# adaLN sums: half of the products moved from VectorE to ScalarE, their additions to GpSimd

## The chip, the cores and the metric

One NeuronCore of a Trainium2 chip runs the whole program. The metric is the device time of one execution in microseconds. Three executions of the kernel before took 2615.36, 2617.19 and 2618.43 us. Besides these, one execution was recorded by the hardware profiler.

The engines are named as in the profile: PE is TensorE (PEld its weight loads), DVE is VectorE, ACT is ScalarE, POOL is GpSimd, SP is SyncE, whose queue issues all the DMA transfers spoken of here.

## The reference

Two layers of a diffusion backbone work on 1024 latent tokens and 256 context tokens, 1024 features each. The part that the change touches is the modulation of each layer by a condition:

```
def _adaln(cond, w, b):
    m = jax.nn.silu(cond) @ w + b
    shift, scale, gate = jnp.split(m[:, None, :], 3, axis=-1)
```

There are two conditions: `c` for the latent tokens and `c_ctx` for the context tokens. The matrix `w_mod` of a layer is 1024 x 3072. So each adaLN product is two rows times a large matrix, a sum over 1024 rows of weights for 3072 columns, twice. The first layer then multiplies the normalised tokens by a matrix of 1024 x 7696 (`w_in_ab`), whose columns feed windowed attention and a bidirectional matrix memory (mLSTM) with its gates, and a second layer follows with latent attention.

## The kernel before, in words

The program's first 60 us compute the shift and scale of layer 0 and the modulated tokens, transposed, as a high and a low part (`hTh`, `hTl`), since a product of 32-bit numbers is made of three matmuls of reduced form. Then PE runs the dense projections block by block (`Dense`, `DenseBlock`, `Unit`): a block is 256 columns of `w_in_ab`, and a unit is one output tile of it, 24 matmuls (8 steps over the 1024 features, three matmuls each) into one PSUM bank, tile `S`. The blocks in the stretch of interest are, in order: the values and gate columns (`a_values`, 10 units with 272 columns, up to 90 us), two blocks of the first memory head that are convolved (`qk_block`: units of 512 and 256 tokens, 90 to 161 us), its values (`v_split`, from 161 us) and its output gates (`o_tanh`, from 195 us).

The weights of a block are split before use: `DenseBlock.split` lets ACT cast a weight tile to the high part `wh` (L354), and POOL subtracts to get the low part `wl` (L355). A block has eight `wl`. Twelve buffers exist (`bufs` 6, times two), so the first four `wl` of a block are made while the block before still runs, and the last four wait until it is nearly done with its own. They fall at the transition from block to block.

The rest of adaLN that does not need to be early (layer 0's gate, layer 1's shift and scale) is computed beside these blocks by `mod_steps`, in six column groups of 512. For each group, eight weight tiles of 128 x 512 (`mw`, four buffers, loaded by SP) are multiplied with one condition value per partition and summed into `macc`, which has a half for each condition: `cd` 0 is `c`, `cd` 1 is `c_ctx`. The first tile is a multiplication (L319), each further one a multiply-and-add on DVE (L321), once for each condition. At the end a matmul with two selecting columns adds up the 128 partitions (`total`), and DVE adds the bias (`bmod`, L306). `Dense.stream` advances this one step for every matmul unit or so. Two groups run beside `a_values` and the first convolved block (67 to 100 us), four beside the next three blocks (150 to 220 us). Later in the program four more groups of 256 columns are summed by the same function.

Between the two, `gates` turns the gate columns (`gt`) into the memory's scaling vectors: a logarithm's series on DVE, transposes of `GI` and `GF` on PE, four kinds of scan along the tokens on DVE (L1371 to L1378), the vectors `LF` and `LI` (L1400, L1401), exponentials on ACT (L1406 to L1413), and transposes of `LI`, `rst` and `gM` back on PE (L107).

In this part of the program the order of the instructions on each engine is set by the framework's scheduler, which plans with its own assumed durations; each engine then works its own list strictly in order and waits where an input is not there. From about 235 us on the order is the program's own (`manual_schedule`).

Of the kernel before, what the change touches and what calls it, by code (L numbers as in the profile page):

```python
# [10 lines left out]
F32 = mybir.dt.float32  # L11
# [3 lines left out]
ALU = mybir.AluOpType  # L15
# [128 lines left out]
def body(tc, I, O, dbg=None, stop_at=None):  # L144
    K = Kern(tc, I, O, dbg)
    with ExitStack() as ctx:
        K.const = ctx.enter_context(tc.tile_pool(name="const", bufs=1))
        K.dram = ctx.enter_context(tc.tile_pool(name="dram", bufs=1, space=DRAM))
        K.left = lambda n: tc.alloc_tile_pool(name=n, bufs=1, side="left", reuse_waits="tile")
        K.right = lambda n: tc.alloc_tile_pool(name=n, bufs=1, side="right", reuse_waits="tile")  # L150
        K.set_psum(S=6, T=2)
        setup_consts(K)
        layer_ab(K)
        layer_c(K)
        K.set_psum()
# [130 lines left out]
def mod_steps(K, p, blocks, ahead, width=512):  # L286


    nc = K.nc
    parts = [(l, f, k) for l, f in blocks for k in range(KD)]  # L290
    asked = []

    def ask():
        if parts:
            l, f, k = parts.pop(0)
            w = K.t(p, [128, width], F32, "mw", ahead)
            K.dma(w, K.I["w_mod"][l, k * 128:(k + 1) * 128, f:f + width])
            asked.append(w)

    def total(l, f, acc):  # L300
        ps = K.ps()
        for cd in range(2):
            K.mm(ps[0:2, 0:width], K.sel[cd], acc[:, cd], cd == 0, cd == 1)
        bm = K.t(p, [2, width], F32, "bmod", 1)
        K.dma(bm, K.I["b_mod"][l:l + 1, f:f + width].to_broadcast([2, width]))
        nc.vector.scalar_tensor_tensor(bm, ps[0:2, 0:width], 0.5, bm, ALU.mult, ALU.add)  # L306
        K.dma(K.modd[l][:, f:f + width], bm)

    for _ in range(ahead):
        ask()  # L310
    late = None
    for l, f in blocks:
        acc = K.t(p, [128, 2, width], F32, "macc", 2)
        for k in range(KD):
            w = asked.pop(0)
            for cd in range(2):
                c = K.condT[:, cd * KD + k:cd * KD + k + 1]
                if k == 0:
                    nc.vector.tensor_scalar(acc[:, cd], w, c, None, ALU.mult)  # L319
                else:  # L320
                    nc.vector.scalar_tensor_tensor(acc[:, cd], w, c, acc[:, cd], ALU.mult, ALU.add)  # L321
            ask()
            if late and k == 5:
                late()
                late = None
            yield
        late = partial(total, l, f, acc)
    if late:
        late()
# [320 lines left out]
def layer_ab(K):  # L650
    nc, I = K.nc, K.I
# [36 lines left out]
    dense = Dense(blocks)  # L688
# [47 lines left out]
    zs[3].parts = 4  # L736
    mp = left("mod")
    dense.mods = mod_steps(K, mp, mods[0:2], 4)
    K.tp = gtp = left("gtmp")
    dense.run(1, 1)  # L740
# [4 lines left out]
    mp.release()  # L745
    mp = left("mod1")
    dense.mods = mod_steps(K, mp, mods[2:], 4)
    dense.run(3, 0.9)
    for _ in dense.mods:
        pass  # L750
    mod_cols(K, 1, mp)
# [5 lines left out]
    w = I["w_out_ab"][0]  # L757
# [40 lines left out]
    p = left("wo2")  # L798
# [1114 lines left out]
def layer_c(K):  # L1913
# [23 lines left out]
    nc.vector.tensor_scalar(ncol[:, 0:3], ps[:, 0:3], QSC, None, ALU.mult)  # L1937
    nc.vector.tensor_copy(ncol[:, 3:5], ps[:, 3:5])
    dense.mods = mod_steps(K, cm, [(1, 2 * D + f) for f in range(0, D, 256)], 4, 256)
    dense.run(3, 0.8)  # L1940
    for _ in dense.mods:
# [412 lines left out]
```

## Time and profile before

| | |
|---|---|
| median of three executions | 2617.19 us |
| profiled execution, its time | 2614.64 us |
| its span in the profile | 2612.8 us |
| granted TensorE clock, mean | 0.997 |
| instructions | 48325 |

The span is the time from the first to the last recorded instruction; 1.8 us of the profiled execution's time lie outside it. Times of rows count from the span's start. In a row of the timeline stand the start, the length, the engine, the line, the operation with its output and inputs, and how many instructions it merges; in square brackets how long the engine had been idle before and what ended this. A row of the windows gives for one stretch the busy time of each engine with the number of its instructions, the clock, and the share of the DMA engines. A row of the waits names the waiting engine and line, what it waited for, the total, the number of times and the longest.

### The profile page before, as it was taken

What the parts mean: (1) busy time and instruction counts of PE and PEld (TensorE: products, weight loads), DVE (VectorE), ACT (ScalarE), POOL (GpSimd) and SP (SyncE); (2) the same over time, 40 slices, a digit from 0 to 9 for tenths busy, and PEclk for the clock granted to TensorE, in tenths of its full rate; (3) what the DMA queues carried; (4) which work ended last, traced back from release to release, by engine and by line L of the source; (5) the groups of instructions that cost most, each with busy time, mean ns of one, the idle gap of its engine ahead of it and who ended that gap; (6) DMA issues with size and microseconds to landing.
All of it is one profiled execution on the core that took longest, in us unless ns stands there. A gap on an engine that the chain in (4) does not pass through costs nothing. (4 is left out here: it accounts for less than half of the span.)

```text
span 2612.8 us, 48325 instructions
## 1 busy us (share of the span) xinstructions
PE 2563.6 (98%) x16233; PEld 2259.4 (86%) x16233; DVE 1779.5 (68%) x4045; ACT 1411.7 (54%) x3608; POOL 1161.8 (44%) x1549
## 2 busy tenths in 40 slices
PE   7999999999999999999999999999999999999998
PEld 6888898898898888887888878898899989999887
DVE  6994565656647676477777546526788888888754
ACT  5232444444434433477666433234788888888842
POOL 4342333423324344356445453224455545555832
PEclk9999999999999999999999999999999999999999
DMA  7565576566667664445443453523310101101333
GB/s 249 155 183 174 163 208 189 160 197 188 179 199 212 204 211 153 135 150 161 120 126 106 130 193 133 160 73 101 88 36 27 45 27 38 36 28 29 120 99 131
DMA packets 352970, 347.23 MB, mean 133 GB/s; under 512 B 36073, under 2 KB 297878, under 8 KB 352466
## 3 DMA queue, kind: packets, MB, share of 16 engines
q1 hardware_dynamic: 352722, 344.14, 43.2%
q8 instruction: 129, 2.11, 0.3%
q14 instruction: 119, 0.97, 0.1%
HBM read 233.52 MB, written 110.51 MB: 132 GB/s over the span
## 5 line engine op out<-in xcount | busy, mean ns | idle before, releaser
L355 POOL TENSOR_TENSOR wl<-wf,wh 128x256 fp32r<-128x256 f32 (+3 forms) x288 | 241.7, 864 | 435.8 <-ACT wh L354 381.2
L103 PE MATMUL mm<-hTh,wh 128*128 128x512 f32 (+1 forms) x912 | 329.0, 361 | 0.9 <-DVE scr L621 0.9
L103 PE MATMUL mm<-hTh,wl 128*128 128x512 f32 (+1 forms) x912 | 325.1, 356 | 0.0
L103 PE MATMUL mm<-hTl,wh 128*128 128x512 f32 (+1 forms) x912 | 325.0, 356 | 0.0
L103 PE MATMUL S<-cK,cQ 96*128 96x512 f32 (+3 forms) x1248 | 296.9, 364 | 2.2 <-ACT cPa L2256 1.3
L2304 DVE TENSOR_TENSOR cpl<-T,cph 128x512 fp32r<-128x512 f32 x336 | 228.6, 686 | 45.9 <-ACT cph L2303 42.8
L103 PEld LDWEIGHTS S<-cK,cQ 96*128 96x128 f32 (+1 forms) x1248 | 193.3, 189 | 25.4 <-ACT cPa L2256 3.5
L2303 ACT CAST cph<-T 128x512 fp32r<-128x512 f32 x336 | 192.4, 591 | 29.8 <-PE T L107 18.6
L103 PEld LDWEIGHTS mm<-hTh,wl 128*128 128x128 f32 x912 | 171.7, 188 | 26.6
L103 PEld LDWEIGHTS mm<-hTh,wh 128*128 128x128 f32 x912 | 171.6, 188 | 24.9 <-DVE scr L621 1.1
L103 PEld LDWEIGHTS mm<-hTl,wh 128*128 128x128 f32 x912 | 171.7, 188 | 23.2
L2254 DVE TENSOR_REDUCE cmx<-S 128x1 f32<-128x512 f32 x256 | 173.2, 682 | 16.7 <-PE S L103 15.2
L103 PE MATMUL V<-cph,cV 128*128 128x256 f32 x672 | 177.2, 290 | 1.1 <-DVE co L2319 0.8
L103 PE MATMUL V<-cpl,cV 128*128 128x256 f32 x672 | 172.1, 284 | 0.3 <-DVE cpl L2304 0.3
L1174 ACT CAST att_ph<-mm 128x512 fp32r<-128x512 f32 x168 | 98.6, 587 | 102.0 <-PE mm L107 100.7
L2235 POOL TENSOR_SCALAR cPa<-cPa,cst 128x512 f32<-128x512 f32 x128 | 98.7, 771 | 118.2 <-DVE cst L2232 97.6
L354 ACT CAST wh<-wf 128x256 fp32r<-128x256 f32 (+3 forms) x288 | 101.8, 409 | 74.9 <-DMA wf<-in_w_in_ab 42.8
L103 PE MATMUL mm<-wh,hTh 128*128 128x256 f32 x480 | 136.9, 285 | 4.0 <-DVE scr L1488 4.0
L1175 DVE TENSOR_TENSOR att_pl<-mm,att_ph 128x512 fp32r<-128x512 f32 x168 | 115.8, 689 | 34.8 <-ACT att_ph L1174 29.2
L1163 POOL TENSOR_SCALAR att_p<-att_p,att_den 128x640 f32<-128x640 f32 (+1 forms) x128 | 97.4, 774 | 86.9 <-DVE att_den L1160 39.1
L103 PE MATMUL mm<-wl,hTh 128*128 128x256 f32 x480 | 135.3, 282 | 0.1
L103 PE MATMUL mm<-wh,hTl 128*128 128x256 f32 x480 | 135.3, 282 | 0.0
(456 smaller groups left out, 7887.6 us busy)
## 6 DMA issues: line engine op xcount, KB each, us to landing
wf<-in_w_in_ab SPq DMA_DIRECT2D x120, 256.0 KB
in<-in SPq DMA_DIRECT2D x40, 514.0 KB
in<-in SPq DMA_DIRECT2D x32, 386.0 KB
mw<-in_w_mod SPq DMA_DIRECT2D x48, 256.0 KB
in<-scr SPq DMA_DIRECT2D x40, 258.0 KB
o_x<-y SPq DMA_DIRECT2D x20, 512.0 KB
wm<-in_w_mod SPq DMA_DIRECT2D x16, 512.0 KB
in<-cx SPq DMA_DIRECT2D x32, 256.0 KB
```

The lines of the kernel that those rows point to most:

```text
L103: return self.nc.tensor.matmul(out, lhsT, rhs, start=start, stop=stop)
L354: K.nc.scalar.copy(wh, wf[:, k])
L355: K.nc.gpsimd.tensor_sub(wl, wf[:, k], wh.bitcast(F32))
L1163: nc.gpsimd.tensor_scalar(pv, pv, den[:, i:i + 1], 1.0, ALU.mult, ALU.mult)
L1174: K.nc.scalar.copy(ph, self.T)
L1175: K.nc.vector.tensor_sub(pl, self.T, ph.bitcast(F32))
L2235: nc.gpsimd.tensor_scalar(pv, pv, wt[:, c:c + 1], rd, ALU.mult, ALU.mult)
L2254: nc.vector.tensor_reduce(mx[:, b, c:c + 1], S, AX.X, ALU.max, negate=True)
L2303: nc.scalar.copy(ph, T_)
L2304: nc.vector.tensor_sub(pl, T_, ph.bitcast(F32))
```

## The change

In `mod_steps`, for groups of 512 columns and from the second weight tile on, the second condition's multiply-and-add on DVE becomes two instructions: ACT multiplies the weight tile by the condition's value into a new tile `mq` (two buffers), and POOL adds `mq` to `macc`. The first condition stays on DVE, and so do the first tiles and the groups of 256 columns. The second hunk changes only a blank. All lines behind the change have numbers higher by four.

```diff
                 if k == 0:
                     nc.vector.tensor_scalar(acc[:, cd], w, c, None, ALU.mult)
+                elif cd == 0 or width < 512:
+                    nc.vector.scalar_tensor_tensor(acc[:, cd], w, c, acc[:, cd], ALU.mult, ALU.add)
                 else:
-                    nc.vector.scalar_tensor_tensor(acc[:, cd], w, c, acc[:, cd], ALU.mult, ALU.add)
+                    q = K.t(p, [128, width], F32, "mq", 2)
+                    nc.scalar.mul(q, w, c)
+                    nc.gpsimd.tensor_add(acc[:, cd], acc[:, cd], q)
...
-    dense.run(3, 0.9)
+    dense.run(3,0.9)
```

In the built program 42 multiply-and-adds (six groups, seven tiles) leave DVE's list, and 42 `ACTIVATE` and 42 `TENSOR_TENSOR` enter ACT's and POOL's. The scheduler also moves other instructions. Three places matter. In the rows a number behind a tile's name tells its buffers apart.

The first is POOL's list around the start of the first convolved block, where the last four `wl` of that block are made (`wl_763` to `wl_775`). Before, they follow the clearing of the gate vectors:

```order
L1368 MEMSET gB 36x1280
L1369 MEMSET gM 36x1280
L355 TENSOR_TENSOR wl_763<-wf_750,wh_762 128x256
L355 TENSOR_TENSOR wl_767<-wf_750,wh_766 128x256
L355 TENSOR_TENSOR wl_771<-wf_760,wh_770 128x256
L355 TENSOR_TENSOR wl_775<-wf_760,wh_774 128x256
```

Now:

```order
L325 TENSOR_TENSOR macc_906<-macc_906,mq_1264 128x512
L325 TENSOR_TENSOR macc_1284<-macc_1284,mq_1319 128x512
L325 TENSOR_TENSOR macc_1284<-macc_1284,mq_1358 128x512
L325 TENSOR_TENSOR macc_1284<-macc_1284,mq_1473 128x512
L325 TENSOR_TENSOR macc_1284<-macc_1284,mq_1492 128x512
L325 TENSOR_TENSOR macc_1284<-macc_1284,mq_1550 128x512
L325 TENSOR_TENSOR macc_1284<-macc_1284,mq_1574 128x512
L325 TENSOR_TENSOR macc_1284<-macc_1284,mq_1611 128x512
L359 TENSOR_TENSOR wl_763<-wf_750,wh_762 128x256
L359 TENSOR_TENSOR wl_767<-wf_750,wh_766 128x256
L359 TENSOR_TENSOR wl_771<-wf_760,wh_770 128x256
L359 TENSOR_TENSOR wl_775<-wf_760,wh_774 128x256
```

All fourteen additions of the first two groups (the last eight are shown) stand between the clearing and `wl_763`. On ACT the fourteen products stand ahead of the casts that make `wh_762` to `wh_774`.

The second is PE's list around the first transpose of the gates' result, `LI`, which DVE makes at the end of the scans. Before, it stands in the second convolved block (its weights are `wh_1202` and on):

```order
L103 MATMUL S_1720<-hTh_131,wl_1207 128x512
L103 MATMUL S_1720<-hTh_131,wh_1212 128x512
L103 MATMUL S_1720<-hTl_132,wh_1212 128x512
L107 MATMUL T_1474<-small,LI 128x36 x10
L103 MATMUL S_1720<-hTh_131,wl_1213 128x512
L103 MATMUL S_1720<-hTh_131,wh_1216 128x512
L103 MATMUL S_1720<-hTl_132,wh_1216 128x512
```

Now it stands 40 rows earlier, in the last unit of the first convolved block:

```order
L103 MATMUL S_1614<-hTh_133,wl_763 128x256
L103 MATMUL S_1614<-hTh_133,wh_766 128x256
L103 MATMUL S_1614<-hTl_134,wh_766 128x256
L107 MATMUL T_1496<-small,LI 128x36 x10
L103 MATMUL S_1614<-hTh_133,wl_767 128x256
L103 MATMUL S_1614<-hTh_133,wh_770 128x256
L103 MATMUL S_1614<-hTl_134,wh_770 128x256
```

Every row of PE below it can start only when `LI` is there. The transposes of `rst` and `gM` move up by 43 rows, the first of `GI` by 16 and the first of `GF` by 35.

The third is POOL's list at the transition to the memory's values, where the last four `wl` of that block are made. Before (`cx` is a convolution's middle tap):

```order
L1465 TENSOR_SCALAR cx_1753<-scr_1713,cw 128x512
L1465 TENSOR_SCALAR cx_1762<-scr_1749,cw 128x512
L1465 TENSOR_SCALAR cx_1807<-scr_1803,cw 128x256
L1465 TENSOR_SCALAR cx_1889<-scr_1848,cw 128x512
L1465 TENSOR_SCALAR cx_1898<-scr_1885,cw 128x512
L355 TENSOR_TENSOR wl_1660<-wf_1647,wh_1659 128x256
L355 TENSOR_TENSOR wl_1664<-wf_1647,wh_1663 128x256
L355 TENSOR_TENSOR wl_1668<-wf_1657,wh_1667 128x256
L355 TENSOR_TENSOR wl_1672<-wf_1657,wh_1671 128x256
```

Now the same four are called `wl_1688` to `wl_1700`:

```order
L1469 TENSOR_SCALAR cx_1843<-scr_1839,cw 128x256
L325 TENSOR_TENSOR macc_1916<-macc_1916,mq_1992 128x512
L325 TENSOR_TENSOR macc_1916<-macc_1916,mq_2068 128x512
L325 TENSOR_TENSOR macc_1916<-macc_1916,mq_2104 128x512
L1469 TENSOR_SCALAR cx_1931<-scr_1888,cw 128x512
L325 TENSOR_TENSOR macc_1916<-macc_1916,mq_2140 128x512
L1469 TENSOR_SCALAR cx_1940<-scr_1927,cw 128x512
L359 TENSOR_TENSOR wl_1688<-wf_1675,wh_1687 128x256
L359 TENSOR_TENSOR wl_1692<-wf_1675,wh_1691 128x256
L325 TENSOR_TENSOR macc_1916<-macc_1916,mq_2166 128x512
L359 TENSOR_TENSOR wl_1696<-wf_1685,wh_1695 128x256
L359 TENSOR_TENSOR wl_1700<-wf_1685,wh_1699 128x256
```

Twelve additions of the third and fourth group (four of them shown) now stand between the first convolution `cx` of the second block and `wl_1688`, and a thirteenth between `wl_1692` and `wl_1696`. PE's list first uses these four 11, 10, 22 and 22 rows later than before.

## The prediction

> **What bounds the kernel now.** I read the page's busy times first, then a table of stretches, then PE's waits, then single rows. PE is busy almost throughout, so a change pays only by what it does to PE's waits and clock.
>
> ```profile
> PE 2563.6 (98%) x16233; PEld 2259.4 (86%) x16233; DVE 1779.5 (68%) x4045; ACT 1411.7 (54%) x3608; POOL 1161.8 (44%) x1549
> ```
>
> The products lie between 67 and 220 us. The windows of that stretch (columns: stretch, length, PE, PEld, DVE, ACT, POOL, clock, DMA share, GB/s):
>
> ```profile
> 70.00:94.00 24.00, 24.00 (x177) 23.08 (x176) 22.72 (x49) 4.44 (x13) 4.17 (x4) 1.00 0.86 260
> 124.00:146.00 22.00, 17.96 (x104) 14.45 (x103) 20.65 (x35) 8.24 (x14) 17.99 (x11) 0.97 0.33 83
> 146.00:168.00 22.00, 22.00 (x135) 19.68 (x135) 21.18 (x38) 4.24 (x10) 7.15 (x7) 0.96 0.61 171
> 168.00:194.00 26.00, 24.64 (x189) 21.93 (x188) 22.57 (x46) 7.85 (x22) 8.48 (x8) 1.00 0.78 238
> ```
>
> DVE is nearly full there and ACT and POOL have room. Yet PE waits little: these are all of its waits from 60 to 260 us.
>
> ```profile
> PE T L107 <- ACT rst L1410: 2.2, 1, 2.2
> PE T L107 <- DVE LI L1401: 1.6, 1, 1.6
> PE S L103 <- POOL wl L355: 0.2, 1, 0.2
> PE S L103 <- DVE bmod L306: 1.4, 1, 1.4
> ```
>
> They make 5.4 us, and one has a sequel. The timeline around the two gate transposes:
>
> ```profile
> 132.18 0.40 PE L103 MATMUL S<-hTl,wh 128*128 128x512 f32 x1
> 134.19 0.78 PE L107 MATMUL T<-small,LI 36*128 36x36 f32 x10 [1.61 <-DVE LI L1401]
> 140.12 0.28 PE L103 MATMUL S<-hTh,wh 128*128 128x256 f32 x1
> 140.24 0.28 PE L103 MATMUL S<-hTl,wh 128*128 128x256 f32 x1
> 142.76 0.80 PE L107 MATMUL T<-small,rst 36*128 36x36 f32 x10 [2.23 <-ACT rst L1410]
> 145.07 0.41 PE L103 MATMUL S<-hTl,wh 128*128 128x256 f32 x1
> 145.28 0.41 PE L103 MATMUL S<-hTh,wl 128*128 128x256 f32 x1
> 148.10 0.39 PE L103 MATMUL S<-hTh,wl 128*128 128x512 f32 x1
> ```
>
> Before the wait for `rst` matmuls of 256 start 0.12 us apart, behind it 0.21; from about 144.5 to 147.9 us the array ran at about half rate, which costs half of 3.4 us, 1.7 us. So everything that this stretch can give back is 5.4 + 1.7 = 7.1 us. That is the bound on the good side.
>
> **The change: the durations.** Rows for each kind of work: DVE's multiply-and-adds, a POOL addition of 128x512 and an ACT activation of that shape elsewhere in the program, and four meetings of POOL with DVE.
>
> ```profile
> L321 DVE SCALAR_TENSOR_TENSOR macc<-mw,condT,macc x84: 728/747/1303, 70.2 to 218.9; 128x512 f32<-128x512 f32 x84
> 70.21 3.39 DVE L321 SCALAR_TENSOR_TENSOR macc<-mw,condT,macc 128x512 f32<-128x512 f32 x5
> L909 POOL TENSOR_TENSOR w<-w,o_x x38: 1273/1292/1680, 1525.8 to 2595.5; 128x512 f32<-128x512 f32 x38
> L1471 ACT ACTIVATE scr<-cx x48: 416/632/637, 107.6 to 707.0; 128x512 f32<-128x512 f32 x32, 128x256 f32<-128x256 f32 x16
> 223.75 2.80 POOL L355 TENSOR_TENSOR wl<-wf,wh 128x256 fp32r<-128x256 f32 x4 [12.77 <-ACT wh L354]
> 89.55 4.17 POOL L355 TENSOR_TENSOR wl<-wf,wh 128x256 fp32r<-128x256 f32 x4 [20.76 <-ACT wh L354]
> 89.95 3.17 DVE L321 SCALAR_TENSOR_TENSOR macc<-mw,condT,macc 128x512 f32<-128x512 f32 x3
> ```
>
> Five multiply-and-adds in a row take 3.39 us, 0.67 each from start to start, so the 42 taken from DVE are worth 42 x 0.67 = 28 us of DVE. ACT gets 42 x 0.63 = 26 us, POOL 42 x 1.29 = 54 us, and both have room for it on average. But POOL and DVE hold each other up: four `wl` alone take 0.70 us each (223.75), beside DVE's sums 1.04 (89.55), and DVE's sums there 1.06 instead of 0.67. One of each takes 1.05 us per pair against 0.70 + 0.67 = 1.37 in sequence: 0.32 us overlaps, the rest excludes the other. For an addition of 512 beside a sum I work out a pair of 1.29 + 0.67 - 0.32 = 1.64 us. So an addition lasts between 1.29 us (DVE elsewhere) and about 1.64 us (DVE summing), and DVE is held up by up to 1.64 - 0.67 = 0.97 us for each product that it saved 0.67 on. Where DVE is busy throughout, the move frees nothing of it.
>
> The Trainium skill, "SBUF — State Buffer", section "Who interferes with whom", says that a VectorE instruction with two SBUF inputs and a GpSimd instruction that reads SBUF share a read port, and that the later one is blocked for the whole of the other. The trace agrees that they exclude each other, but 1.05 us per pair is less than the sum of both. By the rule as written a pair here would last 1.96 us; what that gives is the third rival below.
>
> **First transition, 90 us: no wait.** PE's first need of a late `wl` is this one:
>
> ```profile
> 93.46 0.39 PE L103 MATMUL S<-hTh,wl 128*128 128x512 f32 x1
> ```
>
> The fourteen additions can begin when the first products do, at about 70 us. They last 14 x 1.29 = 18 to 14 x 1.64 = 23 us, so POOL is free for `wl_763` between 88 and 93 us, and it is there by 94. The scheduler has moved PE's use of it behind five more matmuls of 0.23 us, to 94.6. I take no wait; up to 1.5 us is possible, since ACT's casts of `wh` stand behind the products, and each product behind the addition two before it.
>
> **The gates: 2.0 us lost.** DVE's chain to `LI` and `rst`:
>
> ```profile
> 95.03 0.17 DVE L921 COPY gt<-S 128x16 f32<-128x16 f32 x1
> 97.51 0.86 DVE L1320 TENSOR_TENSOR gt<-gt,gb 128x160 f32<-128x160 f32 x1
> 98.29 1.22 DVE L321 SCALAR_TENSOR_TENSOR macc<-mw,condT,macc 128x512 f32<-128x512 f32 x1
> 115.51 4.68 DVE L1378 TENSOR_TENSOR_SCAN gM<-LF,m,LI 4x1024 f32<-4x1024 f32 x2
> 132.03 2.02 DVE L1401 TENSOR_TENSOR LI<-LI,gB 36x1280 f32<-36x1280 f32 x1
> 139.93 1.47 DVE L1409 TENSOR_TENSOR rst<-LI,dl 36x1280 f32<-36x1280 f32 x1
> 141.43 1.27 ACT L1410 ACTIVATE rst<-rst 36x1280 f32<-36x1280 f32 x1
> ```
>
> With sums gone from DVE's list ahead of L1320, it can follow the last gate copy (95.03) closely, 2.3 us earlier; the sum at 98.29 goes (1.2 us); and four steps of the convolution, waits with them, now stand behind the scans or behind `LI` (about 2.5 us). `LI` is then ready 6 us earlier, at 128 instead of 134. PE gets there too early, though: the 40 rows by which its transposes moved up are seven matmuls of 256, some 32 of 512 and one group's total (7 x 0.12 + 32 x 0.23 + 1.8 = 10 us), and before, PE had reached them at 132.4. So it comes at about 122 us, waits 128 - 122 = 6.0 us, and a slow stretch of 1.7 us follows. `rst` needs five more steps of DVE and is there about 7 us behind `LI`, at 135; PE, with 19 matmuls of 512, seven of 256, a total and the slow stretch between, comes at 137 and does not wait. So 6.0 + 1.7 = 7.7 us replace 0.2 + 1.6 + 2.2 + 1.7 = 5.7: 2.0 us more. From below: if DVE comes a further 6 us earlier, all waits vanish, 5.7 us gained; from above, if additions eat DVE's gain (none of the first 2.3 us, 2 more lost), 4 us more, 6.0 lost.
>
> **The transition at 161 us: 5.2 us lost.** SP's first loads for the third group, its first sum, and POOL, ACT and PE at the transition:
>
> ```profile
> 147.43 1.84 SPq L138 DMA_DIRECT2D mw<-in_w_mod  x4
> 152.20 1.41 DVE L321 SCALAR_TENSOR_TENSOR macc<-mw,condT,macc 128x512 f32<-128x512 f32 x2
> L1465 POOL TENSOR_SCALAR cx<-scr,cw 128x512 f32<-128x512 f32 x32 | 28.0, 877 | 31.4 <-ACT scr L1450 19.9 <-PE S L103 7.6 <-DVE scr L1458 2.1
> 158.80 1.33 ACT L354 CAST wh<-wf 128x256 fp32r<-128x256 f32 x4
> 160.25 4.33 POOL L355 TENSOR_TENSOR wl<-wf,wh 128x256 fp32r<-128x256 f32 x4
> 160.87 0.28 PE L103 MATMUL S<-wh,hTh 128*128 128x256 f32 x1
> 164.91 0.28 PE L103 MATMUL S<-wl,hTh 128*128 128x256 f32 x1
> ```
>
> Here POOL is just in time today: its fourth `wl` ends at 160.25 + 4.33 = 164.6, and PE takes it at 164.9. The loads of the third group stand on SP behind the gates' stores, so they too start some 6 us earlier, at 141.4, and the first addition 4.8 us later, at 146.2. Then twelve additions and four `cx` must pass before the first `wl`: 12 x 1.29 + 4 x 0.88 = 19.0 us at the least, 12 x 1.64 + 3.5 = 23.2 us beside DVE's sums. With 0.7 to 1.1 us for itself the first `wl` is there between 166 and 170.5. PE wants it 26 rows of 0.12 us behind the block's start, at 160.9 + 3.1 + 2.0 (the loss above) = 166.0; the last two `wl` stand behind one addition more and come 1 us late again at the dear end. The wait lies between nothing and 5 us; I take 3.5 us, nearer the dear end, because DVE is full in that window (21.18 of 22 us). A wait longer than the 2.2 us seen before also brings the slow stretch, 1.7 us.
>
> For the slow stretch the skill's "TensorE: Matmul & The Clock Gate", section "Part 1: The HAM clock gate (the "warmup" mystery)", asks for an idle window of about 3.4 us; this trace shows one behind a gap of 2.4 us. By the rule the 1.7 us here would be left out, and the forecast would be 1.7 us lower.
>
> **The rest.** ACT's products stand ahead of casts that free PE's banks; six banks of 3 us a unit cover a few us: nothing. SP now issues the loads of the third and fourth group in one run, past the next block's weights, which were asked for here:
>
> ```profile
> 165.66 0.57 SPq L138 DMA_DIRECT2D wf<-in_w_in_ab  x1
> ```
>
> PE wants that block at 195 us; the loads are released four by four by the products, so `wf` may come 5 to 10 us later: hidden, and if it were not, each us late is a us lost. The wait for the bank that `bmod` releases (1.4 us, at 177) goes, since PE arrives some 4 us later and DVE has fewer sums: -1.4 us. At 195 and 229 us the `wl` stand behind casts that wait for PE itself, and the additions ahead of them have 10 us of an idle POOL: nothing; if that cover failed, up to 2 us each. The totals of the groups follow their last addition by several units: nothing. From 235 us on the order is unchanged.
>
> **Sum.** 2.0 + 3.5 + 1.7 - 1.4 = +5.8 us. The profiled execution took 2614.6 us, 1.8 more than its span; it would take 2620.4. It lies 2.6 us under the median of 2617.2, so I forecast a median of 2623.0 us.
>
> **Rivals.** First, faster: DVE runs through gates and convolutions so much earlier that no transpose waits, and POOL keeps up at 1.29 us. For it speaks DVE's full row at 70 to 94 us, against it that 42 additions hold up DVE for as long as it saved. It decides for faster once `LI` is ready before 122 us. Then -7.1 + 1 = -6 us: 2611.
>
> Second, a draw: POOL is late at 161 us by less than a microsecond, with no slow stretch, and the gates come out 1 to 3 us worse: about +2, 2619. The spread of an addition's time allows it.
>
> Third, far worse: each POOL addition and DVE sum exclude each other for their whole length, 1.96 us a pair. Then twelve additions take 23.5 us, `cx` 1.5 each, and a `wl` 1.4: the first `wl` comes at 177, PE waits 11 us, and with 1.7 us slow and 4 at the gates, less 1.4, the loss is 15 us: 2632. The 1.05 us per pair at 89.55 speaks against it. That the change does not do what it says is excluded by the lists: 42 sums left DVE's.
>
> **Chances.** Forecast 0.42, faster 0.13, draw 0.33, far worse 0.12. What this measurement can tell from no change is about 0.2%, 5.2 us. Of the forecast's case, whose own range is 2620 to 2628, about 0.07 falls under that bound. So slower 0.42 - 0.07 + 0.12 = 0.47, same 0.33 + 0.07 = 0.40, faster 0.13. The range reaches from the faster rival to the far worse: 2611 to 2632.
>
> **What would show it.** Right: `macc` on POOL lasts 1.3 to 1.7 us; PE's longest wait is for `LI`, 5 to 8 us; a second for `wl` near 165 us, 2 to 5 us; the clock falls in both windows; from 235 us on all rows are shifted alike. Wrong: `LI` is ready before PE asks, or PE never waits for POOL, or a wait appears at 94 us, where I put none; a difference behind 235 us would mean that I missed a mechanism.

## The result, and the profile after

| | before | after |
|---|---|---|
| median of four executions each | 2617.69 us | 2635.68 us |
| lowest to highest | 2615.36 to 2618.43 | 2635.07 to 2637.19 |
| profiled execution, its span | 2612.8 us | 2633.9 us |
| granted clock, mean | 0.997 | 0.993 |

The ratio is 1.0069, with a 95% interval of 1.0056 to 1.0081. The kernel became slower by 18 us. The forecast was 2623.0, in a range of 2611 to 2632: the direction was right, and the loss was three times as large as forecast, outside the range.

The windows of the changed kernel, in the columns shown before (stretch, length, PE, PEld, DVE, ACT, POOL, clock, DMA share, GB/s):

```profile
70.00:94.00 24.00, 23.42 (x172) 22.28 (x172) 23.69 (x30) 11.63 (x23) 19.74 (x14) 1.00 0.70 218
94.00:124.00 30.00, 25.10 (x118) 18.10 (x117) 25.05 (x60) 9.33 (x24) 12.02 (x13) 0.94 0.37 114
124.00:146.00 22.00, 18.20 (x100) 13.46 (x99) 20.51 (x36) 8.57 (x16) 12.41 (x11) 0.92 0.18 41
146.00:168.00 22.00, 22.00 (x120) 18.86 (x119) 16.19 (x20) 7.49 (x12) 13.27 (x10) 1.00 0.64 183
168.00:194.00 26.00, 12.73 (x79) 10.60 (x78) 24.77 (x34) 10.91 (x23) 21.19 (x18) 0.74 0.59 158
```

Two things stand in them. DVE is as full as before in the first row, 23.69 of 24 us, though it executes 30 instructions instead of 49. And in the last row PE, which had worked 24.6 of 26 us there, works 12.7. One row each for the whole stretch, up to the same place in the program (before, then after):

```profile
60.00:235.00 175.00, 169.60 (x1106) 147.01 (x1105) 144.91 (x278) 44.45 (x109) 63.64 (x55) 0.98 0.55 163
```

```profile
60.00:256.00 196.00, 173.44 (x1102) 148.42 (x1101) 147.88 (x234) 71.89 (x151) 118.88 (x97) 0.94 0.49 145
```

DVE has 44 instructions fewer in this stretch and is busy 3 us longer. POOL is busy 55 us more, ACT 27 us. Behind this stretch nothing changed: from 256 to 621 us PE is busy 363.76 of 365 us, and from 235 to 600 before, 363.75.

The tiles `macc` and `mq` (count, then shortest, median and longest in ns, first and last start) tell why DVE gained nothing:

```profile
L325 POOL TENSOR_TENSOR macc<-macc,mq x42: 1283/1620/1878, 69.4 to 231.8; 128x512 f32<-128x512 f32 x42
L321 DVE SCALAR_TENSOR_TENSOR macc<-mw,condT,macc x42: 734/1570/1885, 70.0 to 228.7; 128x512 f32<-128x512 f32 x42
L324 ACT ACTIVATE mq<-mw,condT x42: 705/724/732, 68.1 to 230.1; 128x512 f32<-128x512 f32 x42
```

The 42 sums that stayed on DVE take 1.57 us each instead of 0.75. Two sums in sequence on DVE alone took 1.34 us (0.67 from start to start). Beside additions on POOL DVE's operations start 1.70 us apart (its rows from 162 us on stand below), so one sum and one addition side by side hold DVE longer than two sums alone.

PE's waits from 60 to 262 us:

```profile
PE S L103 <- ACT wh L358: 13.1, 2, 12.5
PE T L107 <- DVE LI L1405: 3.8, 1, 3.8
PE T L107 <- DVE scr L1458: 2.4, 1, 2.4
PE T L107 <- issue: 1.8, 1, 1.8
PE S L103 <- POOL wl L359: 1.4, 4, 0.7
```

They sum to 22.5 us, against 5.4 before. The wait for `rst` and the one for `bmod` are gone. The two spans differ by 21.1 us; what the waits (17.1) leave, 4 us, is work at a lower clock: in the two long rows above PE is busy 3.8 us longer for the same matmuls. Its granted clock is about 0.5 in three stretches in which it works (100.0 to 103.4, 134.2 to 137.6 and 182.3 to 185.4 us), against one before (144.5 to 147.9). More than half of the loss is one wait of 12.5 us, at the transition to the memory's values, for a cast of `wh` on ACT. Here are, in turn, PE's rows around it, ACT's from 163 us to the cast, and DVE's from 162 to 169 us:

```profile
169.51 0.28 PE L103 MATMUL S<-wh,hTl 128*128 128x256 f32 x1
182.29 0.80 PE L103 MATMUL S<-wh,hTh 128*128 128x256 f32 x2 [12.51 <-ACT wh L358]
182.89 0.41 PE L103 MATMUL S<-wl,hTh 128*128 128x256 f32 x1
183.10 0.41 PE L103 MATMUL S<-wh,hTl 128*128 128x256 f32 x1
```

```profile
163.82 0.63 ACT L1475 ACTIVATE scr<-cx 128x512 f32<-128x512 f32 x1 [2.62 <-DVE cx L1473]
164.35 1.34 ACT L324 ACTIVATE mq<-mw,condT 128x512 f32<-128x512 f32 x2
166.68 0.72 ACT L324 ACTIVATE mq<-mw,condT 128x512 f32<-128x512 f32 x1 [0.98 <-POOL macc L325]
170.99 0.63 ACT L1475 ACTIVATE scr<-cx 128x512 f32<-128x512 f32 x1 [3.58 <-DVE cx L1473]
171.52 0.36 ACT L1454 COPY scr<-S 128x256 f32<-128x256 f32 x1
171.77 0.72 ACT L324 ACTIVATE mq<-mw,condT 128x512 f32<-128x512 f32 x1
175.07 1.41 ACT L324 ACTIVATE mq<-mw,condT 128x512 f32<-128x512 f32 x2 [2.57 <-DMA mw<-in_w_mod]
179.34 0.42 ACT L1475 ACTIVATE scr<-cx 128x256 f32<-128x256 f32 x1 [2.87 <-DVE cx L1473]
...
181.84 1.31 ACT L358 CAST wh<-wf 128x256 fp32r<-128x256 f32 x4
```

```profile
162.01 1.77 DVE L1473 SCALAR_TENSOR_TENSOR cx<-scr,cw,cx 128x512 f32<-128x512 f32 x1
163.71 1.78 DVE L321 SCALAR_TENSOR_TENSOR macc<-mw,condT,macc 128x512 f32<-128x512 f32 x1
165.41 1.78 DVE L1472 SCALAR_TENSOR_TENSOR cx<-scr,cw,cx 128x512 f32<-128x512 f32 x1
167.12 1.77 DVE L321 SCALAR_TENSOR_TENSOR macc<-mw,condT,macc 128x512 f32<-128x512 f32 x1
```

The casts wait for their turn on ACT: the last load of weights (`wf`) ahead of them was issued at 147.28, and before the change they started at 158.80, 2.1 us ahead of the block, which begins at 168.20 here. They stand in ACT's list behind 13 products, and behind three activations of convolutions (L1475) that wait 2.6, 3.6 and 2.9 us for DVE. DVE, which was full from 154 us on, is slow there: not only its sums but also steps of the convolution that meet an addition (L1472, L1473) take 1.77 us instead of 0.74. Of the 24 such steps of 512 columns in the stretch, five are stretched beyond 1.3 us. ACT also waits for POOL (`mq` has two buffers) and for loads of `mw`, which SP issues only when DVE and ACT have let a buffer go. Its waits from 154 to 184 us:

```profile
ACT mq L324 <- DMA mw<-in_w_mod: 9.3, 2, 6.8
ACT scr L1475 <- DVE cx L1473: 9.1, 3, 3.6
ACT mq L324 <- POOL macc L325: 3.8, 4, 1.4
```

The 6.8 us are the wait for the third group's first load, at 154 us, where DVE and POOL stand idle too (5.2 and 6.8 us). Four engines wait for each other, each in order, and the casts that PE needs are the last in the row. Behind the wait PE's matmuls start 0.21 us apart up to 185.5, and 0.12 from there on: 3.2 us at half rate, worth 1.6.

To compare places, I count in each trace from the last `mrow` transposes, the start of the first block, since the stretch up to there took 57.4 to 61.1 us in the profiled executions. Before and after:

```profile
57.62 0.28 PE L107 MATMUL S<-small,mrow 2*128 2x2 f32 x2 [3.25 <-ACT mrow L262]
```

```profile
57.42 0.28 PE L107 MATMUL S<-small,mrow 2*128 2x2 f32 x2 [3.24 <-ACT mrow L262]
168.20 0.28 PE L103 MATMUL S<-wh,hTh 128*128 128x256 f32 x1
```

The memory's values begin 160.87 - 57.62 = 103.3 us behind it before, and 168.20 - 57.42 = 110.8 after: 7.5 us are lost in the first part (transition at 90, gates; one more stretch at half rate, at 100 us, is among them), and the other 13.8 of the 21.3 us behind.

### The profile page after: what moved, and what is told of

It is laid out like the page before. It is cut to its first block, busy times and chain, and to the rows that moved or that the text cites. A ratio compares the mean times of both kernels' runs of the same rounds, so it can differ in the third digit from the quotient of the medians.

```text
span 2633.9 us, 48417 instructions
## 1 busy us (share of the span) xinstructions
PE 2567.7 (97%) x16233; PEld 2261.1 (86%) x16233; DVE 1781.2 (68%) x4003; ACT 1437.9 (55%) x3650; POOL 1220.5 (46%) x1591
## 5 line engine op out<-in xcount | busy, mean ns | idle before, releaser
L103 PEld LDWEIGHTS V<-cph,cV 128*128 128x128 f32 x672 | 126.6, 188 | 7.9 <-DVE co L2323 1.3
```

What stands on the lines that cost most here:

```text
L103: return self.nc.tensor.matmul(out, lhsT, rhs, start=start, stop=stop)
```

## The experiments

The theory that these rows suggest is called interlock: POOL's additions and DVE's operations hold each other up, so DVE is not freed, and what queues behind it in order (convolutions, then ACT's casts) comes late. Its rivals are: order (the scheduler's new lists are themselves the loss), ACT's queue (products ahead of the casts, whatever POOL does), and loads or buffers.

### One part of the change alone

`first_two`: the change in the first two groups alone.

```diff
-                elif cd == 0 or width < 512:
+                elif cd == 0 or width < 512 or len(blocks) == 4:
```

> The change is made only in the first two groups (67 to 100 us); the last four are as before. The engines' lists are those of the changed kernel up to the end of the second convolved block, and those of the kernel before behind it. If the loss adds up place by place, this kernel keeps the changed kernel's stalls of PE at 92 to 97 us (3.6 us in all), at the GF transposes (2.5) and at LI (4.0) with their slow stretches (about 3), and saves the 6 us that the gates cost before: +5 to +9 us against before, so 2623 to 2627 us, and no wait for a cast of wh near 170 us. If the whole loss is the 12.5 us wait at 170 us, it is within 2 us of before. If the first groups only shift work that the third transition then pays for, a wait over 5 us appears at 165 to 180 us though no products are there.

`last_four`: in the last four groups alone.

```diff
-                elif cd == 0 or width < 512:
+                elif cd == 0 or width < 512 or len(blocks) == 2:
```

> The change is made only in the last four groups (150 to 230 us). PE's list is that of before up to the start of the memory's values. If the loss adds up place by place: PE waits 10 to 13 us for a cast of wh at about 165 us, and the time is +12 to +16 us against before, 2629 to 2633 us; with first_two it sums to the changed kernel's +18 within 2 us. If the wait at 170 us needs the lateness that the first groups brought (loads late, gates late), it is under 6 us here and the time below 2625.

| | median | ratio to before, 95% | in us of 2617 |
|---|---|---|---|
| `first_two` | 2622.91 | 1.0023 (1.0013 to 1.0033) | +6.0 |
| `last_four` | 2635.46 | 1.0068 (1.0051 to 1.0084) | +17.8 |
| the whole change | 2635.68 | 1.0069 (1.0056 to 1.0081) | +18.1 |

The first part alone costs about what was expected (5 to 9 us), with waits for `GF` (1.6) and `LI` (3.8). Not expected was a wait of 2.6 us for the late casts at 174 us, where no product stands in ACT's list at all. ACT's waits from 150 to 176 us show that a late DVE reaches the casts by the convolutions alone:

```profile
ACT scr L1475 <- DVE cx L1473: 15.8, 3, 9.4
```

DVE is not held up by additions there: its sums take 0.74 us, but it had waited 4.9 us for the third group's first load and does the sums ahead of the convolutions' steps. So part of the lateness at this transition comes of loads and order, with no addition beside it.

The last four groups alone cost as much as the whole change. I had expected the two parts to sum to the whole within 2 us; by these figures they sum to 23.8 us, not 18.1. The intervals (2.6, 4.3 and 3.3 us to each side) are too wide to exclude the sum, but the waits do stand at other places. The waits of `last_four`, and SP's from 196 to 216 us:

```profile
PE S L103 <- ACT wh L358: 10.9, 2, 7.2
PE S L103 <- POOL wl L359: 2.8, 4, 1.1
```

```profile
SPq L138 <- DVE scr L1492: 11.2, 3, 4.5
```

The wait for casts is there, but in two pieces: 3.7 us at the same transition and 7.2 us at the next one, at 208 us, which costs nothing in the changed kernel. Only seven products stand ahead of the first late cast here, not 13. Together (10.9 us) the two are nearly the 13.1 of the changed kernel, paid at other places. In the second piece it closes through SP: the stores that wait for DVE's results (`scr`, L1492) stand ahead of the loads of `mw` for which ACT's product waits, with the cast behind it.

### The sums left out, and what PE's list makes of it

`no_second`: the second condition's products are left out from the second tile on.

```diff
-                    q = K.t(p, [128, width], F32, "mq", 2)
-                    nc.scalar.mul(q, w, c)
-                    nc.gpsimd.tensor_add(acc[:, cd], acc[:, cd], q)
+                    pass
```

> The second condition's products from the second weight tile on are left out altogether (42 products, so its shift, scale and gate are sums over one tile of eight): DVE loses 42 sums, and ACT and POOL get nothing. PE's list is nearly that of the changed kernel (transposes of GF and LI moved up). Theory interlock (DVE was not freed since additions on POOL and sums on DVE hold each other up, and ACT's casts queue behind products that wait for them): sums on DVE take 0.7 us again, no wait for wh near 170, LI ready before 126 us; time between 2609 and 2618, that is 0 to 8 us less than before. Theory order (the scheduler's new order is itself the loss): PE still waits 4 us at LI and 2.5 at GF, and the time is +3 to +8. Theory products on ACT or additions on POOL are harmless and loads of weights set the pace: the wait near 170 stays above 6 us.

`no_second_late`: besides, the weave of gates and units is given 14 for 10.

```diff
-    weave(gates(K, gp, gtp, gt), 5, dense.stream(1, 1), 10)
+    weave(gates(K, gp, gtp, gt), 5, dense.stream(1, 1), 14)
```

> As no_second (the second condition's 42 sums left out), and the weave of gates and dense units is given 14 for 10, which sets the transposes of LI 26 rows later on PE and those of rst 21 rows later, 16 rows ahead of where they stand in the kernel before. In no_second LI was ready 7.5 us earlier than before, and PE came 9 us earlier and waited 3.6 us. Theory order (the gain of a lighter DVE was handed back by the list of PE): no wait for LI, rst or GF over 1 us, and 4 to 6 us less than no_second: 2609 to 2613. Theory that something else ends the waits: waits of 3 us or more remain at the transposes and the time is 2614 to 2619.

`no_second` took 2616.03 us, ratio 0.9997 (0.9988 to 1.0006): DVE loses 28 us of work, nobody gets it, and the time does not change. `no_second_late` took 2614.93, ratio 0.9985 (0.9976 to 0.9994), 3.9 us less. So in the two lists tried, leaving the work out altogether wins some 4 us at most; a move of it should not win more. The gates in `no_second`:

```profile
58.69 0.28 PE L107 MATMUL S<-small,mrow 2*128 2x2 f32 x2 [3.24 <-ACT mrow L262]
127.80 1.18 PE L107 MATMUL T<-small,LI 36*128 36x36 f32 x10 [3.48 <-DVE mp L1397]
```

and in the changed kernel:

```profile
133.62 0.86 PE L107 MATMUL T<-small,LI 36*128 36x36 f32 x10 [3.80 <-DVE LI L1405]
```

Counted from `mrow`, the transposes of `LI` could start at 134.19 - 57.62 = 76.6 us before, and at 69.1 with the sums left out: DVE is 7.5 us earlier. PE, though, arrives 9 us earlier too, since the scheduler had put these transposes 42 rows higher for a lighter DVE, and it waits 3.5 us. With the transposes 26 rows lower the wait is 2.4 us and that for `GF` is gone. In the changed kernel they start at 76.2, only 0.4 us earlier than before: there DVE's gain does not exist, while PE arrives 2.6 us earlier. The theory of order holds for the gates, at a price of some 3 us, and not for the rest, since `no_second` has nearly the changed kernel's list on PE and no loss. `no_second_late` was expected to lose its waits altogether and did not; its time was 1.9 us above the expected range.

### The additions left out, moved, or made one-input

`no_adds`: products on ACT, but only the last addition of each group.

```diff
-                    nc.gpsimd.tensor_add(acc[:, cd], acc[:, cd], q)
+                    if k == KD - 1:
+                        nc.gpsimd.tensor_add(acc[:, cd], acc[:, cd], q)
```

> As the changed kernel, all 42 products on ACT, but only the last of seven additions per group is made on POOL, so 36 are left out (the second condition's sums lack six of eight tiles). Theory interlock by the additions: DVE's sums fall back to about 0.75 us, ACT's products wait for loads only, the casts of wh come in time: no wait over 2 us near 170, time within 4 us of no_second (2609 to 2620). Theory ACT's queue (casts stand behind products whatever POOL does): the wait for wh near 170 us stays above 6 us and the time is 2625 or more.

`adds_on_dve`: the additions on DVE.

```diff
-                    nc.gpsimd.tensor_add(acc[:, cd], acc[:, cd], q)
+                    nc.vector.tensor_add(acc[:, cd], acc[:, cd], q)
```

> As the changed kernel, products on ACT, but all 42 additions on DVE: POOL is out of it, DVE has as many two-input operations as before the change. Theory exclusion (it is POOL beside DVE that stretches both): sums and additions take 0.65 to 0.8 us each, what stays is ACT's queue as in no_adds (a wait for wh of about 5 us): 2620 to 2626. Theory ACT's queue alone (any late addition holds the products and with them the casts): wait for wh of 8 us or more, 2628 to 2636. The transposes of LI and rst stand 20 rows later than in the changed kernel, close to before, so the gates should cost as before within 2 us.

`one_input`: POOL does an operation of the same size that reads one tile.

```diff
-                    nc.gpsimd.tensor_add(acc[:, cd], acc[:, cd], q)
+                    nc.gpsimd.tensor_scalar(acc[:, cd], q, 1.0, None, ALU.mult)
```

> As the changed kernel, but POOL's 42 additions are replaced by a multiplication of mq with 1.0 written to macc, which reads one tile and not two (the second condition's sums then hold only the last tile). If what stretches both sides is that POOL and DVE read two inputs each: DVE's sums go back to a median of 0.75 to 0.9 us, POOL's operation takes 0.7 to 0.9 us, and the time is that of no_adds, 2620 to 2625. If any POOL operation on these tiles beside a sum holds both: sums above 1.1 us, POOL's above 1.2 us, wait for wh above 8 us, 2628 or more.

`one_input_dve`: POOL's additions as in the change, but DVE's sums in the groups of 512 read one tile.

```diff
-                    nc.vector.scalar_tensor_tensor(acc[:, cd], w, c, acc[:, cd], ALU.mult, ALU.add)
+                    if width < 512:
+                        nc.vector.scalar_tensor_tensor(acc[:, cd], w, c, acc[:, cd], ALU.mult, ALU.add)
+                    else:
+                        nc.vector.tensor_scalar(acc[:, cd], w, c, acc[:, cd, 0:1], ALU.mult, ALU.add)
```

> The changed kernel, in which DVE's 42 sums of the first condition read one tile instead of two: w times c plus the first column of macc (so that condition's sums are not accumulated). POOL's 42 additions stay as they are, in the same places; PE's list is the changed kernel's up to the memory's values, and ACT's and POOL's differ in few rows (12 products instead of 13 ahead of the late casts of wh), while in one_input only 8 stood there. Theory exclusion (an addition with two inputs on POOL and a sum with two inputs on DVE hold each other up): POOL's additions fall from 1.62 to about 1.3 us, DVE's sums to about 0.5, the late cast of wh comes 10 us or more earlier than in the changed kernel, counted from the last mrow transposes (110 to 115 us behind them, not 124.9), the wait of PE falls from 12.5 to under 5 us, the time is 2619 to 2625. Theory queues (thirteen products ahead of the casts, and POOL's own 1.3 us an addition, make the cast late whatever DVE does): sums fall but the wait stays above 8 us, 2628 or more.

The measured times, with the median of POOL's operation and of DVE's sum, the number of products that ACT's list has between the third group's start and the late cast, the time at which PE had that cast (from `mrow`), and PE's wait for it:

| | POOL | DVE sum | products ahead | cast | wait | median | ratio, 95% |
|---|---|---|---|---|---|---|---|
| the change | 1.62 | 1.57 | 13 | 124.9 | 12.5 | 2635.68 | 1.0069 (1.0056 to 1.0081) |
| `no_adds` | none | 0.75 | 14 | 111.2 | 5.2 | 2623.06 | 1.0016 (1.0006 to 1.0026) |
| `adds_on_dve` | none | 0.74 | 7 | 108.2 | 2.9 | 2621.79 | 1.0014 (1.0005 to 1.0023) |
| `one_input` | 1.50 | 0.75 | 8 | 111.3 | 1.3 | 2623.50 | 1.0016 (1.0007 to 1.0026) |
| `one_input_dve` | 1.35 | 1.10 | 12 | 117.7 | 8.4 | 2627.68 | 1.0042 (1.0025 to 1.0059) |

`no_adds` and the change differ in 36 additions alone and have nearly the same lists: the 36 additions cost 0.0053, 14 us. `no_adds` and `no_second` differ in the 42 products and the six additions kept: these cost 0.0019, 5 us. So the products in ACT's queue are a cause too, the smaller one. Its rows in `no_adds`, PE's wait and ACT's from 146 to 172 us:

```profile
PE S L103 <- ACT wh L359: 5.2, 1, 5.2
```

```profile
ACT mq L324 <- DMA mw<-in_w_mod: 14.2, 8, 6.6
```

Here the products wait for loads, not for POOL, and hold the casts; for DVE's convolutions ACT waits 0.8 us, where it waited 9.1 in the changed kernel. The theory that the wait goes with the additions (expected: under 2 us) failed on this point; the theory of the queue alone (2625 or more) failed as well.

Is it POOL's time that the additions cost, or their hold on DVE? In `one_input` POOL is busy as long, 21.16 us of the 26 between 168 and 194 us, and each of its operations lasts 1.5 us (0.7 to 0.9 had been expected, which makes the comparison only sharper):

```profile
168.00:194.00 26.00, 23.15 (x166) 20.86 (x165) 17.30 (x35) 11.71 (x27) 21.16 (x19) 0.93 0.60 177
```

```profile
L325 POOL TENSOR_SCALAR macc<-mq x42: 1484/1498/2422, 73.0 to 231.0; 128x512 f32<-128x512 f32 x42
L321 DVE SCALAR_TENSOR_TENSOR macc<-mw,condT,macc x42: 734/752/1294, 73.5 to 226.5; 128x512 f32<-128x512 f32 x42
```

DVE's sums beside it take 0.75 us, DVE is busy 17.3 us there and not 24.8, and the time is that of `no_adds`. The median is no accident of sums that meet nothing: 25 of the 42 have one of these operations, and no two-tile one, beside them for over three tenths of their time; of these the median is 0.75 us too and the longest 1.09. So the loss goes with the hold on DVE and not with POOL's time. One reservation: the lists differ, and the scheduler put eight products ahead of the late cast here, not 13. But `last_four` with seven lost 17.8 us, and `no_adds` with 14 only 4.2, so their number does not decide.

`adds_on_dve` shows it from the other side:

```profile
L321 DVE SCALAR_TENSOR_TENSOR macc<-mw,condT,macc x42: 729/742/1230, 70.2 to 219.2; 128x512 f32<-128x512 f32 x42
L325 DVE TENSOR_TENSOR macc<-macc,mq x42: 668/680/1216, 70.9 to 219.9; 128x512 f32<-128x512 f32 x42
```

A sum and an addition together take 0.74 + 0.68 = 1.42 us of DVE; the sum alone, with the addition on POOL, takes 1.57. DVE is better off doing both. This is what the theory of exclusion expected (2620 to 2626). What is left, +3.7 us, goes with waits for ACT's casts (2.9), `wl` (1.5) and `LI` (3.5).

`one_input_dve` has the changed kernel's lists but for a few rows, and came out between its theories. The wait of 8.4 us is what the theory of queues expected (above 8), the time of 2627.7 lies just under its range (2628 or more) and above that of exclusion (2619 to 2625). POOL's addition is freed of the meeting, as expected (1.35 us for 1.62), but DVE's sum is not:

```profile
L328 POOL TENSOR_TENSOR macc<-macc,mq x42: 1277/1352/1709, 69.9 to 224.3; 128x512 f32<-128x512 f32 x42
L324 DVE TENSOR_SCALAR macc<-mw,condT,macc x42: 529/1103/1612, 70.3 to 221.8; 128x512 f32<-128x512 f32 x42
```

An operation that takes 0.53 us undisturbed takes up to 1.6 beside an addition. That both must read two tiles, as I had it, is wrong on DVE's side: an addition with two tiles on POOL holds up DVE's one-tile sums as well. The run therefore did not take the hold away, and does not separate the two theories by itself. The loss stands between the other cases as the hold does: 1.57 - 0.75 = 0.82 us more per sum costs 18 us, 1.10 - 0.53 = 0.57 costs 11, none costs 4. DVE also has less to do here (0.53 us a sum and not 0.75), though less work on DVE alone gained nothing in `no_second`.

### Buffers, loads, and smaller doses

`more_buffers`: eight `mq` and eight `mw` in the last four groups, four `mq` in the first two.

```diff
-                    q = K.t(p, [128, width], F32, "mq", 2)
+                    q = K.t(p, [128, width], F32, "mq", 4 if len(blocks) == 2 else 8)
...
-    dense.mods = mod_steps(K, mp, mods[2:], 4)
+    dense.mods = mod_steps(K, mp, mods[2:], 8)
```

> As the changed kernel, with eight mq and eight mw buffers in the last four groups (two and four before) and four mq in the first two. The lists keep nearly the changed kernel's order. Theory interlock through few buffers (a product on ACT waits for the addition two before it and for a load that a late sum releases, and the casts wait behind it): ACT runs its products ahead, the wait for a cast of wh near 170 us falls from 12.5 to under 5 us, time 2622 to 2628. Theory throughput (additions and sums exclude each other, about 1.6 us a pair, and no buffer helps): sums and additions keep 1.57 and 1.62 us, the wait stays above 8 us or turns into one for wl on POOL of the same size, time 2631 to 2637.

`no_adds_8_loads`: `no_adds` with the last of these edits.

> As no_adds (all products on ACT, 36 of the 42 additions left out), with eight mw buffers instead of four in the last four groups. In no_adds ACT waited 14.2 us for loads of mw between 146 and 172 us, with the casts of wh behind its products. Theory loads through few buffers: eight loads go out at once, ACT's products run ahead, the wait for wh falls from 5.2 to under 1.5 us, and the time is 3 to 5 us less than no_adds: 2617 to 2620. Theory ACT's queue (the products stand ahead of the casts, and the loads come at the pace of the DMA engines): the wait stays above 3.5 us, 2621 to 2625.

`more_buffers` took 2639.70 us, ratio 1.0077 (1.0060 to 1.0094), even above the range that the theory of throughput gave (2631 to 2637):

```profile
PE S L103 <- ACT wh L358: 15.0, 2, 13.9
```

```profile
L325 POOL TENSOR_TENSOR macc<-macc,mq x42: 1284/1620/1861, 72.0 to 238.7; 128x512 f32<-128x512 f32 x42
L321 DVE SCALAR_TENSOR_TENSOR macc<-mw,condT,macc x42: 732/1568/1780, 72.6 to 230.2; 128x512 f32<-128x512 f32 x42
```

Too few buffers are not the cause: sums and additions stay as long, and with more buffers the scheduler puts 19 products ahead of the casts. `no_adds_8_loads` took 2622.63, ratio 1.0019 (1.0010 to 1.0029), as `no_adds`: PE's wait falls from 5.2 to 3.8 us only, with 18 products ahead of the cast, and ACT still waits 9.8 us for loads there (14.2 before). That speaks for products in ACT's queue that wait for loads, and against the number of load buffers; that 18 stand ahead and not 14 keeps the two from being parted cleanly.

`three_of_seven`: the change for the tiles 2, 4 and 6 of each group.

```diff
-                elif cd == 0 or width < 512:
+                elif cd == 0 or width < 512 or k % 2:
```

> The change for the weight tiles 2, 4 and 6 of each group only: 18 products on ACT and 18 additions on POOL, 24 sums of the second condition stay on DVE. If the loss follows the number of additions that meet sums on DVE, 18/42 of 18 us: +6 to +10 us, 2625 to 2629. If DVE has room to take the fewer stretched sums without a delay at the transition, the wait for wh near 170 is under 3 us and the time is that of first_two or less, up to +5: 2618 to 2623. If any product at all holds the casts, as long as in the changed kernel, +14 or more.

`seed_on_act`: the kernel before, the first tile's two products on ACT, nothing on POOL.

```diff
-                    nc.vector.tensor_scalar(acc[:, cd], w, c, None, ALU.mult)
+                    if width < 512:
+                        nc.vector.tensor_scalar(acc[:, cd], w, c, None, ALU.mult)
+                    else:
+                        nc.scalar.mul(acc[:, cd], w, c)
```

> The kernel before, where only the first tile's two multiplications of each group of 512 move from DVE to ACT (12 operations of 0.48 us); no POOL, no mq: DVE's next sum waits for ACT's product, and ACT's casts stand behind one load of weights per group. DVE is relieved of 6 us in all. Since leaving out 42 sums (28 us) altogether gained 1 us with the list as the scheduler made it and 4 us with later transposes, the gain here is at most 1 us: 2616 to 2620, no change that can be told. If ACT's queue costs as in no_adds wherever a load is late, +2 to +5 us.

`three_of_seven` took 2628.73 us, ratio 1.0037 (1.0024 to 1.0051), +9.7 us. By the dose, 18/42 of 18.1, it would be 7.8; it lies inside the expected 6 to 10. But the agreement shows no more than that: only five of its 66 sums take over 1.3 us, and PE's wait of 5.8 us for `wh` has products ahead that wait 17.5 us for loads (ACT, 150 to 176 us), as in `no_adds`. `seed_on_act` took 2618.40, ratio 1.0003 (0.9994 to 1.0013), no change that can be told. No version here beats the kernel before with all its work done.

## Why the prediction was wrong

**The bound on the good side** was right, and the true bound is tighter: with the sums gone altogether nothing was gained, and 3.9 us with the transposes later in PE's list, not 7.1. So the first rival, faster by 6 us, was out of reach.

**The durations** held, but for one. The addition was put between 1.29 and 1.64 us and took 1.28 to 1.88, 1.62 in the middle. The pair of 1.64 us was nearly right (1.70 from start to start, where sums and additions follow each other): the third rival's whole-length exclusion (1.96) is wrong, though its time, 2632, came nearest. The product on ACT took 0.72 instead of 0.63, 4 us more of ACT in sum, which is small.

**The step that failed first** is that this pair was not carried on. The text said that "where DVE is busy throughout, the move frees nothing of it", and then let DVE be 6 us earlier in every later step: `LI` ready at 128 (it was at 133.6), the first loads of the third group at 141.4 (they were issued at 148.25), the first addition at 146.2 (155.16). It also held the price to DVE's sums alone; some of the convolutions' steps, which feed ACT, are stretched as much, from 0.74 to 1.77 us.

**First transition:** "I take no wait; up to 1.5 us is possible". There were three, 0.6 for `wh`, 0.7 for `wl` and 1.8 before a transpose that the profile puts down to nothing it shows (issue). With `GF` (2.4), which had no term, and `LI` (3.8 where 6.0 stood, PE arriving at 129.8 and not at 122), the first part lost 7.5 us where 2.0 had been summed. That `rst` would not be waited for was right, and so was the slow stretch behind `LI`; the one at 100 us, 1.7 us, had no term. Not all of the 7.5 need be the hold on DVE: from `mrow` to the values `no_adds` lost 162.39 - 57.96 - 103.3 = 1.1 us, and `one_input`, where DVE is not held up, 169.48 - 61.07 - 103.3 = 5.1, with lists of its own. What POOL's occupation alone costs there was not taken apart and stays open.

**The transition at 161 us:** 5.2 us had been summed, of them a wait of 3.5 for `wl`. The wait was 12.5 us, plus 1.6 at half rate (1.7 had been put), and it was not for `wl` on POOL but for `wh` on ACT. The sentence that failed is "ACT's products stand ahead of casts that free PE's banks [...]: nothing". Only the casts that free banks had been looked at, and not the casts of `wh`, four of which stand behind 13 products in the same list. This was to be read in ACT's list before any run. That a wait longer than 2.2 us brings the slow stretch did not hold throughout: behind the wait of 2.4 us for `GF` at 112 us the clock stays at 1.00, and at 100 us it falls behind one of 1.8 us (and two shorter ones just before). (The gap that the prediction puts at 2.4 us is 2.23 us in its row.) POOL was late too, but hidden behind it: its first late `wl` came at 184.3, and PE waited 0.2 to 0.4 us for each of three of them.

**The rest** held: the wait for `bmod` is gone, nothing is lost at 195 and 229 us, and from 235 us on (256 now) all is shifted alike. That the loss waits at whichever transition comes next, as `last_four` has it, was not foreseen.

**The page on the shared port.** The prediction weighed the Trainium skill, "SBUF — State Buffer", section "Who interferes with whom", by which the later of two such instructions is blocked for the whole of the other. (The section calls the shared ports an exclusive lock; the full block it states for VectorE's modes with two ports.) For the change that would give the third rival's 1.96 us from start to start, or 0.73 + 1.28 = 2.01 by the shortest durations; the rows above start 1.70 us apart, and the additions last 1.62. The same section says that a VectorE instruction with two SBUF inputs contends with a GpSimd instruction that reads SBUF, and that one with at most one input, outside the modes with two ports, does not. In `one_input` the first is not borne out on VectorE's side (sums at 0.75 us, at most 1.09, beside an operation of 1.50 that reads one tile). In `one_input_dve` a `tensor_scalar` with one tile is held up (1.10 for 0.53); the section names that operation among those that can enter a mode with two ports, and no run here shows in which mode it ran, so this run neither bears the section out nor contradicts it. Where they differ, the measurements decide.

## What to carry to other kernels

Before work is moved from VectorE to GpSimd, price VectorE's remaining work at its duration beside the moved operation, all of it and not only the neighbours in the same loop: here 0.75 us became 1.57, and moving 28 us freed nothing. Then read, for each engine that gets work, what stands behind it in its list that the bounding engine needs, here four casts of 0.33 us behind 13 products. And first leave the work out altogether and time that: it says about how much a move can win. Here it was nothing (0.9997), and 3.9 us with the transposes set later.

## What was not expected of the hardware

On GpSimd a `tensor_scalar` of 128x512 with the constant 1.0 takes 1.50 us (1.49 where VectorE does nothing beside it), longer than the two-tile addition alone (1.28), while the convolutions' `tensor_scalar` of the same shape took 0.88 on average. Yet it hardly holds up VectorE's two-tile sums, and the shorter addition does, also where VectorE reads one tile. In these runs what GpSimd executes decided, and not how long it lasts. Only these two of its operations were tried, and they differ in kind and in the tiles they read, so which of the two matters stays open.
